# Seven products for seven more pairs of chunks in a first feed-forward, and 2x written into the banks of w_down

## The chip, the cores and the metric

The kernel runs on one core of a Trainium2 chip, without other cores at work. The metric is the device time of one execution in microseconds; the time before is the median of three runs.

TensorE multiplies a 128x128 stationary tile with 512 moving columns into a bank of its accumulation memory (PSUM, eight banks of 128x512 here). VectorE (DVE in the profile) and ScalarE (ACT) prepare operands and empty the banks. SyncE (SP) issues the loads of the weights.

## The reference, cut to what matters

```python
def swiglu(h, w_gate, w_up, w_down):
    return (jax.nn.silu(h @ w_gate) * (h @ w_up)) @ w_down

def reference(...):
    x = x + 0.5 * swiglu(rms_norm(x, ffn1_norm), ffn1_w_gate, ffn1_w_up, ffn1_w_down)
    x = gated_parallel_mixer(x, ...)
    x = memory_cross_attention(x, mem, ...)
    x = x + 0.5 * swiglu(rms_norm(x, ffn2_norm), ffn2_w_gate, ffn2_w_up, ffn2_w_down)
    return rms_norm(x, final_norm)
```

There are 256 tokens of width 2048, and the inner width of a feed-forward is 5632. Everything is float32. The change touches the first feed-forward, and the form of the `w_down` product in both.

## The kernel before

**Three matmuls for a product.** [...] A product of two split tiles is three matmuls (lines 442 to 444: `hi` by `hi`, `hi` by `lo`, `lo` by `hi`). The activations are split once. The weights are split as they come: ScalarE casts a raw tile to `hi` (L365), VectorE subtracts it from the raw tile to get `lo` (L366). `hi` and `lo` have three buffers each.

**Blocks and groups.** The inner width is cut into 11 blocks of 512 columns, numbered 0 to 10. They stand in three groups: blocks 0 to 3, 4 to 7, 8 to 10. A group first computes gate and up of its blocks, and then multiplies its part of the hidden activations with the matching rows of `w_down`, in two calls: output columns 0 to 1023, then 1024 to 2047. The result is added into `x`, which stays in SBUF.

**Pairs of chunks and seven products.** The inner dimension of a product is cut into chunks of 128, and two chunks are a pair. A pair in `product_pair` makes two token halves by two column blocks (gate and up, or two column blocks of `w_down`): eight products. A pair that is named in `seven` uses Winograd's form of Strassen's scheme instead, with seven products `p1` to `p7`. That needs four sums of the raw weight tiles on VectorE (L394 to L397, `raw<-raw`), the split of two tiles of sums (`thi` on ScalarE L373, `tlo` on VectorE L374, one buffer each), and combinations of the activations (`c` for the gate and up blocks, `d` for `w_down`), which a background task (`combinations`, lines 474 to 493) makes ahead. One product goes into each of the banks `p1` to `p7`; the pairs with eight products add into `p2`, `p4`, `p3` and `p5` for the four results. Since the banks of the seven products are shared between the results, a pair with eight products that comes before the last pair with seven must not add into `p5`. The blocks of gate and up get around this with combinations of the activations (`less` in line 555, pairs 1 and 3); `w_down` uses a further bank `q` (`to = "q"`).

Banks come in three rings: `mm` with three (`p1`, `p3`, `p5`), `acc` with three (`p2`, `p4`, `q`) and `tr` with two (`p6`, `p7`, and transposes).

```python
SEVEN, SEVEN_DOWN = (0, 2, 4), ((2, 4, 6), (2, 4))
```

So before, all of the blocks 1 to 10 in the first feed-forward take seven products for pairs 0, 2 and 4 of their eight; `w_down` does so for pairs 2, 4 and 6 in the first call of the two larger groups, and for pairs 2 and 4 otherwise. In the second feed-forward (`SEVEN_2`) it is pairs 0, 2, 3, 4.

**The ends of a block.** When the last pair with seven is done, `middle` combines `p1`, `p6`, `p7`, `p5` (L579 to L581, with `hb` copied by ScalarE in L576). After the last pair of the block, `out` adds each of `p2`, `p4`, `p3`, `p5` as it is finished (L588, Silu on ScalarE in L589, L592, L593): this is called the tail below. The result `hb` of a block is transposed on TensorE (L630) after the next block's `middle`, and split (`hhi` L635, `hlo` L636). For `w_down`, `first`, `middle` and `out` add into `x` (L603, L606, L611 to L613): 12 VectorE instructions and one of ScalarE in a call.

**What sets the order.** The program is written as one stream: `next_item` fetches the two weight tiles of a pair, loads what lies ahead, and splits the next pair as well (`AHEAD`), so that VectorE and ScalarE are one pair ahead of TensorE. A background task advances at each `bg.tick()`. From this stream, a scheduler of the framework makes the order on each engine, within the dependences; each engine then runs its own list strictly in that order. So an instruction that waits holds up what stands behind it on its engine.

## Time and profile before

| | us |
| --- | --- |
| median of three runs (2217.84 to 2219.36) | 2218.06 |
| the profiled execution | 2216.97 |
| its span, first to last instruction | 2215.2 |
| first feed-forward in it, about | 5 to 710 |
| blocks 0 to 3 and their `w_down` | 5 to 180, 180 to 265 |
| blocks 4 to 7 and their `w_down` | 265 to 433, 433 to 518 |
| blocks 8 to 10 and their `w_down` | 518 to 644, 644 to 710 |
| second feed-forward, its first `w_down` starts | 1679 |

The page gives busy times of each engine, then their shares in 40 slices of 55 us. A window gives the same for any stretch. The timeline lists instructions with start and length; on TensorE and VectorE the end of one overlaps the start of the next, so the price of an instruction is the distance between two starts and not its length. The row of a wait names the waiting instruction, what it waited for, the total, the count and the longest.

### The profile page before, as it was taken

The page shows a single profiled execution, that of the slowest core. Times are in us where ns is not written, and L with a number is a line of the kernel's source. Part 1 is how long each engine was busy: PE and PEld are TensorE (multiplying, and loading weights), DVE is VectorE, ACT ScalarE, POOL GpSimd, SP SyncE. Part 2 cuts the span into 40 slices and gives each one's busy share as a digit, 9 for nine tenths or more (in the row PEclk, how much of TensorE's full clock was granted, in tenths as well). Part 3 has the DMA queues.
Part 4 walks back from the last instruction along what each step waited for, and adds up shares of the span by engine and source line. Part 5 has one row for each costly group of instructions (what it writes and reads, how often), then busy time and mean ns, then how long its engine had stood idle before and what let it go on. Part 6 is the DMA issues. An engine that isn't in the chain of part 4 may idle for free.

```text
span 2215.2 us, 28140 instructions
## 1 busy us (share of the span) xinstructions
PE 2200.2 (99%) x10520; PEld 1817.0 (82%) x10520; DVE 1829.0 (83%) x2348; ACT 1250.0 (56%) x1621; POOL 107.0 (5%) x185
## 2 busy tenths in 40 slices
PE   9999999999999999999999999999999999999998
PEld 7888888888888877788888888888888888888886
DVE  7999988898989476977667666558999999999997
ACT  7555555555556477644544546556565565555654
POOL 0000000000000000000331130001000000000000
PEclk9999999999999999999999999999999999999999
DMA  8555555555556545676768687547665666665573
GB/s 306 199 207 198 194 200 201 198 199 194 200 194 204 178 130 165 197 237 210 223 224 287 209 273 270 183 164 280 220 221 190 212 227 211 214 208 208 200 244 135
DMA packets 231560, 466.02 MB, mean 210 GB/s; under 512 B 15520, under 2 KB 17920, under 8 KB 231424
## 3 DMA queue, kind: packets, MB, share of 16 engines
q1 hardware_dynamic: 222256, 438.08, 58.4%
q0 software_dynamic: 7648, 23.52, 3.5%
q10 hardware_dynamic: 1520, 2.63, 0.3%
q8 instruction: 82, 1.34, 0.3%
q14 instruction: 54, 0.44, 0.1%
HBM read 440.49 MB, written 23.59 MB: 209 GB/s over the span
## 4 chain that ended last, share of the span: by engine, by line
PE 94%; DVE 3%; DMA 1%; issue 1%; ACT 1%; SPq 0%; POOLq 0%; POOL 0%; DVEq 0%; ACTq 0%
PE acc L442 19%; PE acc L443 19%; PE acc L444 19%; PE mm L443 8%; PE mm L444 8%; PE mm L442 8%; PE tr L443 2%; PE tr L630 2%; PE tr L442 2%; PE tr L444 2%; PE mm L1425 1%; DVE lo L366 1%; DMA raw<-in_ffn_w_up_dram 1%; PE tr L1355 0%; ACT hi L365 0%
## 5 line engine op out<-in xcount | busy, mean ns | idle before, releaser
L365 ACT CAST hi<-raw 128x1024 fp32r<-128x1024 f32 (+1 forms) x768 | 755.1, 993 | 687.7 <-PE acc L444 485.9
L366 DVE TENSOR_TENSOR lo<-raw,hi 128x1024 fp32r<-128x1024 f32 (+1 forms) x768 | 878.8, 1147 | 291.8 <-ACT hi L365 289.3
L442 PE MATMUL acc<-hi,xhi 128*128 128x512 f32 (+1 forms) x1134 | 445.7, 394 | 2.0 <-DVE ga L1278 1.5
L443 PE MATMUL acc<-lo,xhi 128*128 128x512 f32 (+1 forms) x1134 | 439.9, 388 | 0.8 <-DVE lo L366 0.8
L444 PE MATMUL acc<-hi,xlo 128*128 128x512 f32 (+1 forms) x1134 | 439.7, 388 | 0.0
L442 PEld LDWEIGHTS acc<-hi,xhi 128*128 128x128 f32 x1134 | 213.2, 188 | 47.8 <-issue 3.1
L444 PEld LDWEIGHTS acc<-hi,xlo 128*128 128x128 f32 x1134 | 212.9, 188 | 43.5 <-issue 0.4
L443 PEld LDWEIGHTS acc<-lo,xhi 128*128 128x128 f32 x1134 | 213.4, 188 | 42.7 <-DVE lo L366 2.2
L373 ACT CAST thi<-raw 128x1024 fp32r<-128x1024 f32 x192 | 200.3, 1052 | 69.1 <-DVE raw L396 45.0
L374 DVE TENSOR_TENSOR tlo<-raw,thi 128x1024 fp32r<-128x1024 f32 x192 | 232.1, 1217 | 0.9 <-ACT thi L373 0.3
L442 PE MATMUL mm<-hi,xhi 128*128 128x512 f32 x402 | 156.6, 389 | 0.1
L443 PE MATMUL mm<-lo,xhi 128*128 128x512 f32 x402 | 156.5, 389 | 0.0
L444 PE MATMUL mm<-hi,xlo 128*128 128x512 f32 x402 | 156.4, 389 | 0.0
L444 PE MATMUL acc<-hi,hlo 128*128 128x512 f32 x372 | 145.4, 391 | 0.0
L443 PE MATMUL acc<-lo,hhi 128*128 128x512 f32 x372 | 145.3, 391 | 0.0
L442 PE MATMUL acc<-hi,hhi 128*128 128x512 f32 x372 | 145.0, 390 | 0.0
L442 PEld LDWEIGHTS mm<-hi,xhi 128*128 128x128 f32 x402 | 75.4, 188 | 16.2 <-ACT hi L365 0.5
L443 PEld LDWEIGHTS mm<-lo,xhi 128*128 128x128 f32 x402 | 75.5, 188 | 15.8
L444 PEld LDWEIGHTS mm<-hi,xlo 128*128 128x128 f32 x402 | 75.5, 188 | 15.7
L442 PEld LDWEIGHTS acc<-hi,hhi 128*128 128x128 f32 x372 | 69.9, 188 | 14.3
L443 PEld LDWEIGHTS acc<-lo,hhi 128*128 128x128 f32 x372 | 69.8, 188 | 14.3
L444 PEld LDWEIGHTS acc<-hi,hlo 128*128 128x128 f32 x372 | 69.9, 188 | 14.0
(443 smaller groups left out, 3526.6 us busy)
## 6 DMA issues: line engine op xcount, KB each, us to landing
raw<-in_ffn_w_down_dram SPq DMA_DIRECT2D x88, 1024.0 KB, 5.2
raw<-in_ffn_w_gate_dram SPq DMA_DIRECT2D x84, 1024.0 KB, 5.1
raw<-in_ffn_w_up_dram SPq DMA_DIRECT2D x78, 1024.0 KB, 6.0
raw<-in_w_in_dram SPq DMA_DIRECT2D x136, 512.0 KB, 3.8
raw<-in_w_out_dram SPq DMA_DIRECT2D x32, 512.0 KB, 4.7
raw<-sums SPq DMA_DIRECT2D x20, 512.0 KB, 6.2
raw<-in_w_proj_attn_dram SPq DMA_DIRECT2D x16, 512.0 KB, 4.0
raw<-in_w_proj_rwkv_dram SPq DMA_DIRECT2D x16, 512.0 KB, 5.7
```

Of the source, the lines that this page charges most:

```text
L365: at["hi"] = act.copy(hi[:, s], raw[:, s])
L366: at["lo"] = dve.tensor_tensor(lo[:, s], raw[:, s], f32(hi[:, s]), ALU.subtract)
L373: act.copy(hi[:], v[:])
L374: dve.tensor_tensor(lo[:], v[:], f32(hi[:]), ALU.subtract)
L442: pe.matmul(o, xh, hi, start=first, stop=False, **how)
L443: pe.matmul(o, xh, lo, start=False, stop=False, **how)
L444: pe.matmul(o, xl, hi, start=False, stop=last, **how)
L630: pe.transpose(b[:, o : o + P], tok[:, t, col : col + P], ident[:])
L1425: pe.matmul(vb[to, (o + k) * P : (o + k + 1) * P][:, r], lhs(k, e), v[:, k, r], start=v is u and k + e == 0, stop=True, **ek,)
```

## The change

It has four parts.

1. In the first feed-forward, the blocks 3, 5, 7, 9 and 10 take seven products for pairs 0, 2, 4, 6 (`SEVEN_MORE`), the blocks 4, 6 and 8 for pairs 2, 4, 6 (`SEVEN_LATER`); blocks 1 and 2 keep 0, 2, 4. The second call of `w_down` takes pairs 2, 4, 6 in the two larger groups. Counted: 5 blocks and 2 calls with one seven more, 7 in all. In blocks 4, 6 and 8 it is as many as before, at other pairs.
2. The combinations for pair 6 are made later than the others (from item 26 of the plan on, in block 2), and `combinations` gets the list of pairs with `less` explicitly. A block waits only for the combinations that it uses. A pair with eight products that has no `less` combination (pair 5, and pair 0 in the blocks that start later) adds its `p5` part into the bank `q`, so the eight blocks with pair 6 have one more VectorE instruction in their tail.
3. In `w_down`, in both feed-forwards, ScalarE first writes twice `x` into the banks `p2`, `p4`, `p3` and `q` (`onto`), and the matmuls add to it. `first` is one ScalarE instruction that writes half of `p1` over `x`, and `middle` and `out` are eight VectorE instructions instead of 12. Each call so has four ScalarE instructions more and four VectorE instructions fewer.
4. Two unused tiles (`shift`, `pad`) go, and `down` needs no tiles `u`.

```diff
 SEVEN, SEVEN_DOWN = (0, 2, 4), ((2, 4, 6), (2, 4))
+SEVEN_MORE, MORE = (0, 2, 4, 6), (3, 5, 7, 9, 10)
+SEVEN_LATER, LATER_ON = (2, 4, 6), (4, 6, 8)
...
-                yield (wg, wu), 0, KD, (j * 512, j * 512), SEVEN_2 if last else SEVEN
+                seven = SEVEN_MORE if j in MORE else SEVEN_LATER if j in LATER_ON else SEVEN
+                seven = SEVEN_2 if last else seven
+                yield (wg, wu), 0, KD, (j * 512, j * 512), seven
...
-            yield (wd, wd), 4 * j0, 4 * nj, (1024, 1536), SEVEN_DOWN[1]
+            yield (wd, wd), 4 * j0, 4 * nj, (1024, 1536), SEVEN_DOWN[last or nj < 4]
...
-    def product_pair(x: Act, c, w, first, middle, out):
+    def product_pair(x: Act, c, w, first, middle, out, onto=()):
...
+        for to, there in onto:
+            b[to] = rings[to]()
+            act.activation(b[to][:], there, AF.Copy, scale=2.0)
+            begun.add(to)
...
-                less = to == "p3" and early and c["early"]
-                if to == "p5" and early and not c["early"]:
+                less = to == "p3" and early and q in c["less"]
+                if to == "p5" and early and q not in c["less"]:
                     to = "q"
...
-                dve.tensor_tensor(v[:], b[to][:], v[:], ALU.add)
+                for z in (to, "q") if t and "q" in b else (to,):
+                    dve.tensor_tensor(v[:], b[z][:], v[:], ALU.add)
...
-    def down(sp, h: Act, c, w, xs):
-
-        u2, u3 = sums_of(sp)
-
-        def half(x_, v):
-            dve.scalar_tensor_tensor(x_, v, 0.5, x_, ALU.mult, ALU.add)
+    def down(h: Act, c, w, xs):
+
+        (x00, x01), (x10, x11) = xs
+
+        def half(x_, v, y):
+            dve.scalar_tensor_tensor(x_, v, 0.5, y, ALU.mult, ALU.add)
 
         def first(b):
-            act.copy(u3[:], b["p1"][:])
-            half(xs[0][0], b["p1"][:])
-            half(xs[1][1], b["q"][:])
+            act.activation(x00, b["p1"][:], AF.Copy, scale=0.5)
 
         def middle(b):
-            dve.tensor_tensor(u2[:], b["p6"][:], u3[:], ALU.add)
-            dve.tensor_tensor(u3[:], b["p7"][:], u2[:], ALU.add)
-            dve.tensor_tensor(u2[:], b["p5"][:], u2[:], ALU.add)
-            half(xs[1][0], u3[:])
-            half(xs[1][1], u3[:])
-            half(xs[0][1], u2[:])
+            half(x01, b["p6"][:], x00)
+            half(x10, b["p7"][:], x01)
+            half(x01, b["p5"][:], x01)
+            half(x11, b["q"][:], x10)
...
+        product_pair(
+            h, c, w, first, middle, out, (("p2", x00), ("p4", x10), ("p3", x01), ("q", x11))
+        )
...
-            sp, norm.x, SEVEN_2 if last else SEVEN, "c",
-            lambda: at["item"] > begun + (4 if last else 7) and not (last and norm.r is None),
+            sp, norm.x, SEVEN_2 if last else SEVEN_MORE, "c",
+            lambda q: (
+                at["item"] > begun + (4 if last else 26 if q > 4 else 7)
+                and not (last and norm.r is None)
+            ),
+            less=(1,) if last else (1, 3),
```

In the order that results, two places show what moves. The names end in the number of the tile; the lines of the changed program are a few higher (L366 becomes L368, L588 L594, L592 L599, L593 L600, L636 L642).

VectorE before, at the start of block 7: the last sums and splits of pair 0, the tail of block 6, then the gate's `lo` of pair 1.

```order
L374 TENSOR_TENSOR tlo_3212<-raw_3205,thi_3211 128x1024
L366 TENSOR_TENSOR lo_3216<-raw2_3113,hi_3215 128x1024
L374 TENSOR_TENSOR tlo_3224<-raw_3206,thi_3223 128x1024
L366 TENSOR_TENSOR lo_3220<-raw2_3169,hi_3219 128x512
L588 TENSOR_TENSOR hb_2910<-acc_2935,hb_2910 128x512
L588 TENSOR_TENSOR hb_2910<-acc_2943,u_2912 128x512
L592 TENSOR_TENSOR u_2911<-mm_2939,u_2911 128x512
L592 TENSOR_TENSOR u_2912<-mm_2947,u_2912 128x512
L593 SCALAR_TENSOR_TENSOR hb_2910<-u_2911,rs_450,hb_2910 128x512
L593 SCALAR_TENSOR_TENSOR hb_2910<-u_2912,rs_450,hb_2910 128x512
L366 TENSOR_TENSOR lo_3265<-raw2_3113,hi_3264 128x1024
```

VectorE after, at the same place. Ahead of these rows stand the splits of pair 0 and the first three of the tail and of the block's transposes (two L594, one L642). The last row is again the gate's `lo` of pair 1.

```order
L474 TENSOR_TENSOR raw_3267<-hhi_2250,hlo_2251 128x512
L642 TENSOR_TENSOR hlo_2251<-tr_3260,hhi_2250 128x512
L480 TENSOR_TENSOR raw_3267<-raw_3267 128x128
L482 TENSOR_TENSOR raw_3267<-raw_3267 128x128
L481 TENSOR_TENSOR raw_3267<-raw_3267 128x128
L599 TENSOR_TENSOR u_2938<-mm_2964,u_2938 128x512
L483 TENSOR_TENSOR raw_3267<-raw_3267 128x128
L600 SCALAR_TENSOR_TENSOR hb_2937<-u_2938,rs_448,hb_2937 128x512
L599 TENSOR_TENSOR u_2939<-mm_3020,u_2939 128x512
L493 TENSOR_TENSOR dlo_2253<-raw_3267,dhi_2252 128x512
L599 TENSOR_TENSOR u_2939<-acc_2971,u_2939 128x512
L368 TENSOR_TENSOR lo_3308<-raw2_3140,hi_3307 128x1024
```

Between the splits of pair 0 and the `lo` of pair 1 now also stand the second `hlo` of the transposed block, one whole combination (L474 to L493) and the add of the bank `q` (the last L599); one scaled add of the tail went behind the `lo`.

ScalarE before, at the end of block 3 and the start of `w_down`: casts of weights (`hi`), the two Silu of the tail (L589) and the casts of the transposed block (`hhi`).

```order
L365 CAST hi_1517<-raw2_1425 128x1024
L365 CAST hi_1521<-raw2_1481 128x1024
L589 ACTIVATE hb_1222<-hb_1222,rs_450 128x512 x2
L365 CAST hi_1561<-raw2_1425 128x1024
L635 CAST hhi_146<-tr_1576 128x512
L635 CAST hhi_146<-tr_1581 128x512
L365 CAST hi_1565<-raw2_1481 128x1024
```

ScalarE after, at the same place, with the writes from `x` into the banks `p2`, `p4` (acc_1576, acc_1578) and `q` (acc_1582).

```order
L367 CAST hi_1513<-raw2_1427 128x1024
L641 CAST hhi_144<-tr_1529 128x512
L641 CAST hhi_144<-tr_1534 128x512
L595 ACTIVATE hb_1228<-hb_1228,rs_448 128x512
L367 CAST hi_1517<-raw2_1476 128x1024
L595 ACTIVATE hb_1228<-hb_1228,rs_448 128x512
L515 ACTIVATE acc_1576<-x_106 128x512
L515 ACTIVATE acc_1578<-x_106 128x512
L367 CAST hi_1586<-raw2_1427 128x1024
L490 CAST dhi_146<-raw_1541 128x512
L367 CAST hi_1590<-raw2_1476 128x1024
L515 ACTIVATE acc_1582<-x_106 128x512
```

The writes into `p2` and `p4` stand behind both Silu and ahead of the casts of the second pair of `w_down`; the write into `q` stands behind them and ahead of the casts of the third.

28 lines of the change are left out of this document (13 added, 15 removed).

## The prediction

> **What bounds the kernel now.** I read the page first: busy shares, then the slices, then the waits of TensorE, then the first feed-forward by windows, then single instructions in the timeline.
>
> ```profile
> span 2215.2 us, 28140 instructions
> PE 2200.2 (99%) x10520; PEld 1817.0 (82%) x10520; DVE 1829.0 (83%) x2348; ACT 1250.0 (56%) x1621; POOL 107.0 (5%) x185
> PE   9999999999999999999999999999999999999998
> DVE  7999988898989476977667666558999999999997
> ```
>
> TensorE has work all the time, so an instruction taken from it is worth its full slot. But VectorE has hardly less to do in the first thirteen slices, where the change is made. A window over the first feed-forward and the waits of TensorE say how much room is left:
>
> ```profile
> 50.00:710.00 660.00, 659.68 (x2957) 544.70 (x2956) 605.48 (x752) 369.32 (x421) 1.47 (x2) 1.00 0.57 197
> PE tr L1007 <- DVE s L998: 1.6, 1, 1.6
> PE acc L443 <- DVE lo L366: 0.8, 2, 0.5
> ```
>
> The columns are length, then busy time of TensorE, its weight loads, VectorE, ScalarE, GpSimd, then the granted clock. VectorE is busy 605.5 of 660 us, 92%; TensorE waits for it almost never. It can't run far ahead, though: it writes its `lo` tiles into three buffers and its `tlo` tiles into single ones, so it is one item ahead at most. What counts is the head start: by how much a `lo` tile is ready before the first matmul that reads it.
>
> Prices come from the distances between starts, since the ends overlap. First TensorE, then eight transposes among matmuls, then VectorE at the start of block 7:
>
> ```profile
> 221.64 0.39 PE L444 MATMUL mm<-hi,hlo 128*128 128x512 f32 x1
> ...
> 225.27 0.39 PE L442 MATMUL mm<-hi,hhi 128*128 128x512 f32 x1
> 121.55 1.03 PE L630 MATMUL tr<-ident,hb 128*128 128x128 f32 x8
> 122.66 0.40 PE L443 MATMUL acc<-lo,xhi 128*128 128x512 f32 x1
> 384.72 1.22 DVE L366 TENSOR_TENSOR lo<-raw,hi 128x1024 fp32r<-128x1024 f32 x1
> 385.85 0.68 DVE L397 TENSOR_TENSOR raw<-raw,raw 128x512 f32<-128x512 f32 x1
> 386.46 1.22 DVE L374 TENSOR_TENSOR tlo<-raw,thi 128x1024 fp32r<-128x1024 f32 x1
> 387.59 1.22 DVE L366 TENSOR_TENSOR lo<-raw,hi 128x1024 fp32r<-128x1024 f32 x1
> 388.73 1.22 DVE L374 TENSOR_TENSOR tlo<-raw,thi 128x1024 fp32r<-128x1024 f32 x1
> 389.86 0.68 DVE L366 TENSOR_TENSOR lo<-raw,hi 128x512 fp32r<-128x512 f32 x1
> 390.46 0.68 DVE L588 TENSOR_TENSOR hb<-acc,hb 128x512 f32<-128x512 f32 x1
> 391.06 0.68 DVE L588 TENSOR_TENSOR hb<-acc,u 128x512 f32<-128x512 f32 x1
> 391.66 1.28 DVE L592 TENSOR_TENSOR u<-mm,u 128x512 f32<-128x512 f32 x2
> 392.89 1.41 DVE L593 SCALAR_TENSOR_TENSOR hb<-u,rs,hb 128x512 f32<-128x512 f32 x2
> 394.22 1.22 DVE L366 TENSOR_TENSOR lo<-raw,hi 128x1024 fp32r<-128x1024 f32 x1
> 652.10 0.28 DVE L482 TENSOR_TENSOR raw<-raw 128x128 f32<-128x128 f32 x1
> 652.30 0.29 DVE L481 TENSOR_TENSOR raw<-raw 128x128 f32<-128x128 f32 x1
> ```
>
> - TensorE: 16 matmuls from 221.64 to 225.27, 0.227 us each. A product is three of them, 0.68 us. Eight transposes: 122.66 - 121.55 - 0.23 = 0.88 us.
> - VectorE: 0.60 us for 512 columns (389.86 to 390.46), 1.136 for 1024, 0.66 for a scaled add (392.89 to 394.22 for two), 0.20 for 128.
>
> So an item with eight products ("plain") takes TensorE 24 x 0.227 = 5.44 us and VectorE two `lo`, 2.27 us. An item with seven takes TensorE 4.76 us and VectorE four sums, two `tlo`, a `lo` and half a one: 5 x 0.60 + 3 x 1.136 = 6.42 us. Each new seven thus saves TensorE 0.68 us and costs VectorE 4.15 us.
>
> **The change part by part.**
>
> *Seven pairs.* 7 x 3 = 21 matmuls fewer: -21 x 0.227 = -4.8 us. In the same feed-forward VectorE gets 7 x 4.15 = 29.0 us, one more add in eight blocks (the bank `q`, 8 x 0.60 = 4.8) and the combinations of pair 6 (0.60 + 4 x 0.20 + 0.60 = 2.0); the six calls of `w_down` lose four instructions each (-14.4). Net +21.4 us on 605.5, with TensorE's time 4.8 shorter: about 96%. It fits on average, so the places decide.
>
> *Start of block 7.* The head start at the `lo` that limits there follows by a walk. In the rows above VectorE is ready at 384.72 + 1.22 = 385.94 with the last `lo` of block 6 and at 395.44 with the gate's `lo` of pair 1. TensorE's first uses of the two:
>
> ```profile
> 388.44 0.39 PE L443 MATMUL mm<-lo,xhi 128*128 128x512 f32 x1
> 395.92 0.39 PE L443 MATMUL acc<-lo,xhi 128*128 128x512 f32 x1
> ```
>
> The head start falls from 2.50 to 0.48 us. By prices: 2.50 + 7.48 of TensorE - 9.48 of VectorE = 0.50, so the walk holds. After the change the last seven of block 6 is pair 6, its tail comes late, and VectorE has 22 instructions between the same two tiles: 13 of 512 columns, four of 1024, four of 128 and one scaled add, 7.83 + 4.54 + 0.81 + 0.66 = 13.8 us (seven of them the head of the block, two `hlo`, six of a combination, six of the tail of block 6, the `lo` itself). TensorE has 37 matmuls, 8.4 us. A last `lo` behind a seven and eight transposes has at most this head start, as in block 3:
>
> ```profile
> 162.08 1.21 DVE L366 TENSOR_TENSOR lo<-raw,hi 128x1024 fp32r<-128x1024 f32 x1
> 166.49 0.39 PE L443 MATMUL mm<-lo,xhi 128*128 128x512 f32 x1
> ```
>
> 166.49 - 163.29 = 3.2 us. So 3.2 + 8.4 - 13.8: TensorE waits 2.2 us. Bounds 1.0 and 3.5 (a head start of 4.4, or of 1.9).
>
> *Start of block 10.* The same without the combination and with one sum before the stretch: 12.4 against 8.4 us, 3.2 + 8.4 - 12.4: it waits 0.8 us (0 to 2.1). Blocks 5 and 9 have a plain start of the block ahead of them, and the same walk ends at +0.2 us there.
>
> *Three entries into `w_down`* (behind blocks 3, 7, 10). Today one is already tight:
>
> ```profile
> 191.66 1.22 DVE L374 TENSOR_TENSOR tlo<-raw,thi 128x1024 fp32r<-128x1024 f32 x1
> 192.57 0.39 PE L444 MATMUL mm<-hi,hlo 128*128 128x512 f32 x1
> 192.93 0.50 PE L443 MATMUL tr<-tlo,dhi 128*128 128x512 f32 x1
> 193.27 0.39 PE L444 MATMUL tr<-thi,dlo 128*128 128x512 f32 x1
> ```
>
> The steps 0.36 and 0.34 instead of 0.227 lose 0.25 us. Now two combinations instead of one, the tail and two `hlo` fall between the second `lo` of the call and its first `tlo`: 14 of 512, four of 1024, two scaled adds and eight of 128 columns, 15.9 us, against 12.0 of TensorE (49 matmuls and eight transposes). 3.2 + 12.0 - 15.9 = -0.7; less the 0.25 that is lost already, 3 x 0.47 = +1.4 us (0 to 4).
>
> *ScalarE's writes.* No row shows a write from SBUF into a bank; the nearest are these:
>
> ```profile
> L589 ACT ACTIVATE hb<-hb,rs 128x512 f32<-128x512 f32 x40 | 27.4, 718 | 7.2 <-DVE hb L588 7.2
> L490 ACT CAST dhi<-raw 128x512 fp32r<-128x512 f32 x16 | 10.0, 622 | 16.2 <-DVE raw L483 16.2
> L606 ACT COPY u<-mm 128x512 f32<-128x512 f32 x11 | 6.5, 587 | 10.4 <-PE mm L444 10.4
> ```
>
> I take 0.62 us, the source being SBUF (0.59 to 0.72). 44 of them, 27 us on an engine that is busy 56%, cost nothing as such. But `p2` is the first bank that TensorE fills in a call, and its write waits for VectorE's last read of the bank, behind two Silu and a cast of 1024 columns in ScalarE's queue; casts stand behind it. By walk the write ends 0.3 us before its use and that of `q` as it is needed: 0.2 us each, 3 x 0.2 = +0.6. If the whole chain of 0.72 + 1.05 + 0.72 + 0.62 = 3.1 us were open it would be 9.3; below, 0. The other eight calls (the second halves, and the second feed-forward, whose blocks leave a bank of three free) have over 1.5 us: nothing.
>
> *Tight running.* Pairs 0, 2, 4, 6 leave VectorE 10.2 - 8.7 = 1.5 us in every two items, so after each of these places it stays near 0 for some items. About six more `tlo` come with under 0.25 us; at the 0.25 us lost above that is +1.5 (0 to 5).
>
> *The rest.* The four VectorE instructions that each call in the second feed-forward loses stand behind its tight entry: 0 (at best -1). The removed tiles hold no instruction: 0.
>
> Sum: -4.8 + 2.2 + 0.8 + 1.4 + 0.6 + 1.5 = +1.7 us on the profiled execution of 2216.97 us (span 2215.2 and 1.8 around it). That execution is 1.1 below the median 2218.06, so the median becomes 2219.8; I say 2220.
>
> [...]
>
> **The rivals.**
>
> 1. *Faster: VectorE hides it all.* TensorE loses nothing, 2218.06 - 4.8 = 2213.3. For it: 92% busy, and waits of 0.8 us in the whole run. Against it: the walk at block 7, which needs a head start of 5.4 us where rows show 3.2. Chance 0.09.
> 2. *Slower: the write into `p2` comes late.* From 1 us to the whole 3.1 at the three entries and 0.5 at the other three calls of the first feed-forward: +4.5 to +10.8 in place of 0.6, so 2224 to 2230. It decides once VectorE's last read of the bank slips by over 0.3 us behind the crowded stretch. Chance 0.13.
> 3. *Slower: near 0 throughout.* In blocks 3, 5, 7, 9, 10 each of 20 sevens loses 0.25 us, 5.0 instead of 1.5: 2223.5. For it: ScalarE and VectorE hand tiles to and fro, and the walk has no gap between instructions. Chance 0.11.
> 4. *Slower: an instruction occupies VectorE for its whole duration where it waits for ScalarE's cast each time.* The starts are then 0.68 apart, 22 x 0.08 = 1.8 us more at each of five places: 2229. The spacing at 385 to 394 us speaks against it. [...] Chance 0.06.
> 5. [...] Chance 0.04.
>
> **How the numbers follow.** The forecast has 0.57, with its own range 2216 to 2223. A change under 0.2% (4.4 us, 2213.6 to 2222.5) can't be told from none here. Faster: rival 1, 0.09. Within: the forecast but for 0.02, and half of rival 5, 0.57. Slower: 0.02 + 0.02 + 0.13 + 0.11 + 0.06 = 0.34. The range 2215 to 2226.5 leaves out rival 1, rival 4 and the upper part of rival 2, some 0.2.
>
> **What would show it.** Right: 21 matmuls fewer; VectorE near 96% from 50 to 705 us; waits of TensorE for `lo` and `tlo` of some 6 us in all, the longest, about 2 us, at the start of block 7, some 390 us into the span, others at the three entries. The writes into banks show as 44 ScalarE rows of about 0.6 us. Wrong: TensorE waiting for ScalarE's writes, waits in the second feed-forward, or a longest wait at another place; no waits at all would mean that the head start is larger than the rows say.

## The result and the profile after

The changed kernel takes 2230.62 us (median of four runs, 2229.42 to 2231.1) against 2218.26 us. The ratio is 1.0054, with a 95% interval of 1.0042 to 1.0067: slower by 12.4 us, outside the forecast range (2215 to 2226.5). The profiled execution has a span of 2229.1 us, 13.9 more than before.

The same lines of the page as for the kernel before:

```profile
span 2229.1 us, 28202 instructions
PE 2203.0 (99%) x10499; PEld 1810.8 (81%) x10499; DVE 1836.1 (82%) x2360; ACT 1281.6 (57%) x1680; POOL 107.3 (5%) x185
PE   9999999999999999999999999999999999999998
DVE  7999899998999476978657666558999899998996
```

TensorE has the 21 matmuls fewer (10520 to 10499), and VectorE 7.1 us more work. The busy share of TensorE still reads 99%: in the rows below a matmul is 0.39 us long and the next starts 0.227 us after it, so a wait of a tenth of a us leaves no gap in the record, and the shares don't show the loss. The window over the first feed-forward, and the waits of TensorE:

```profile
50.00:705.00 655.00, 646.22 (x2868) 526.72 (x2867) 611.19 (x771) 384.10 (x451) 1.89 (x3) 1.00 0.59 197
```

```profile
PE acc L444 <- ACT hi L367: 3.0, 4, 0.9
PE acc L445 <- DVE lo L368: 1.7, 3, 0.9
...
PE acc L444 <- DVE hb L594: 1.5, 3, 0.6
...
PE mm L444 <- ACT hi L367: 1.3, 3, 0.4
PE tr L636 <- DVE u L586: 1.2, 1, 1.2
...
PE mm L445 <- DVE lo L368: 1.1, 3, 0.4
```

VectorE is busy 611.2 of 655 us, 93%, where 96% was forecast. Its work came out as forecast (627.0 us from 50 to 722 us, for 605.5 + 21.4); the time did not get shorter. And the waits are not for VectorE's `lo` and `tlo` alone: the longest in total is for ScalarE's casts (`hi`), and reads of banks in the tail (L594) and in `middle` (L586) stand among them.

To place the loss I compare the time from the first matmul with a combination of `x` (in block 1) to the last with `hhi` (in the last call of `w_down`). In the kernel before:

```profile
52.08 0.73 PE L442 MATMUL tr<-thi,chi 128*128 128x512 f32 x2 [0.26 <-ACT thi L373]
...
709.65 0.39 PE L443 MATMUL mm<-lo,hhi 128*128 128x512 f32 x1
```

In the changed kernel:

```profile
53.07 0.73 PE L444 MATMUL tr<-thi,chi 128*128 128x512 f32 x2 [0.26 <-ACT thi L375]
...
720.96 0.39 PE L445 MATMUL mm<-lo,hhi 128*128 128x512 f32 x1
```

That is 657.6 us before and 667.9 after, 10.3 more although 21 matmuls (4.8 us) are gone. So 15.1 us of waits were added in this stretch. The other 3.6 us of the span lie in front of it (1.0) and behind it (2.6), where the profiles of the other kernels differ from the one before by up to 2.2 and by -0.6 to 2.8 us too. Behind it two waits are new in this execution, 1.1 us for `x` (L1612) and 0.9 us for a `tlo` in the second feed-forward; e7's profile has both and e16's neither, so I leave them out and explain only the 15.1. The table of the experiments gives this figure for every kernel ("added waits": difference of that stretch to 657.6, plus 0.227 us for each matmul saved).

TensorE's rows give the places; a wait is the distance of two starts less 0.227 us. At the entry into `w_down` behind block 3:

```profile
193.96 0.39 PE L444 MATMUL mm<-hi,dhi 128*128 128x512 f32 x1
194.18 0.39 PE L444 MATMUL acc<-hi,hhi 128*128 128x512 f32 x1
195.25 0.50 PE L444 MATMUL acc<-hi,hhi 128*128 128x512 f32 x1 [0.68 <-ACT hi L367]
196.12 0.50 PE L445 MATMUL mm<-lo,dhi 128*128 128x512 f32 x1 [0.36 <-DVE lo L368]
196.46 0.40 PE L446 MATMUL mm<-hi,dlo 128*128 128x512 f32 x1
196.69 0.39 PE L444 MATMUL mm<-hi,hhi 128*128 128x512 f32 x1
196.93 0.63 PE L444 MATMUL tr<-thi,dhi 128*128 128x512 f32 x2
197.99 0.49 PE L444 MATMUL mm<-hi,hhi 128*128 128x512 f32 x1 [0.44 <-ACT hi L367]
198.46 0.50 PE L445 MATMUL tr<-tlo,dhi 128*128 128x512 f32 x1
198.79 0.39 PE L446 MATMUL tr<-thi,dlo 128*128 128x512 f32 x1
```

Nine steps (the row at 196.93 holds two matmuls) take 4.61 us from 194.18 to 198.79 instead of 2.04: 2.55 us. The entries behind blocks 7 and 10 lose as much to within 0.05 us. Before, 0.21 to 0.25 us were lost at each, so 3 x 2.3 = 6.9 us are new. The other places, in the same profile:

| place | added, us | what TensorE waits for |
| --- | --- | --- |
| three entries into `w_down` | 6.9 | casts `hi`, then `lo` |
| end of block 6 and start of block 7 | 4.2 | 1.4 at the transposes, 0.5 at a bank of `acc`, 1.1 and smaller for `lo` and sums |
| start of block 10 | 1.0 | a bank of `acc`, freed by the tail |
| start of block 5 | 1.1 | the same |
| all the rest | 1.9 | waits under 0.3 us each |

### The profile page after: what moved, and what is told of

Its sections match the earlier page's. It is cut to its first block, busy times and chain, and to the rows that moved or that the text cites. A ratio compares the mean times of both kernels' runs of the same rounds, so it can differ in the third digit from the quotient of the medians.

```text
span 2229.1 us, 28202 instructions
## 1 busy us (share of the span) xinstructions
PE 2203.0 (99%) x10499; PEld 1810.8 (81%) x10499; DVE 1836.1 (82%) x2360; ACT 1281.6 (57%) x1680; POOL 107.3 (5%) x185
## 4 chain that ended last, share of the span: by engine, by line
PE 87%; DVE 7%; DMA 3%; ACT 1%; issue 1%; SPq 0%; POOLq 0%; POOL 0%; DVEq 0%; ACTq 0%
PE acc L444 18%; PE acc L445 18%; PE acc L446 18%; PE mm L445 7%; PE mm L446 7%; PE mm L444 7%; DVE lo L368 2%; DMA raw<-in_ffn_w_up_dram 2%; PE tr L445 2%; PE tr L446 2%; PE tr L636 2%; PE tr L444 2%; PE mm L1435 1%; ACT hi L367 1%; DVE tlo L376 1%
## 5 line engine op out<-in xcount | busy, mean ns | idle before, releaser
L368 DVE TENSOR_TENSOR lo<-raw,hi 128x1024 fp32r<-128x1024 f32 (+1 forms) x768 | 874.6, 1144 | 280.4 <-ACT hi L367 278.0
L375 ACT CAST thi<-raw 128x1024 fp32r<-128x1024 f32 x206 | 214.8, 1051 | 78.0 <-DVE raw L398 50.8
L376 DVE TENSOR_TENSOR tlo<-raw,thi 128x1024 fp32r<-128x1024 f32 x206 | 249.7, 1219 | 1.2 <-ACT thi L375 0.6
L445 PE MATMUL mm<-lo,xhi 128*128 128x512 f32 x365 | 142.2, 390 | 0.0
L446 PE MATMUL mm<-hi,xlo 128*128 128x512 f32 x365 | 142.1, 389 | 0.0
L444 PE MATMUL mm<-hi,xhi 128*128 128x512 f32 x365 | 141.6, 390 | 0.0
L396 DVE TENSOR_TENSOR raw<-raw,raw 128x512 f32<-128x512 f32 x93 | 63.9, 687 | 33.8 <-DMA raw<-in_ffn_w_up_dram 23.5
L444 PEld LDWEIGHTS mm<-hi,xhi 128*128 128x128 f32 x365 | 68.5, 188 | 14.9 <-ACT hi L367 0.5
L445 PEld LDWEIGHTS mm<-lo,xhi 128*128 128x128 f32 x365 | 68.5, 188 | 14.3
```

The source lines that it names most:

```text
L368: at["lo"] = dve.tensor_tensor(lo[:, s], raw[:, s], f32(hi[:, s]), ALU.subtract)
L375: act.copy(hi[:], v[:])
L376: dve.tensor_tensor(lo[:], v[:], f32(hi[:]), ALU.subtract)
L396: dve.tensor_tensor(t[1][:, 0], ru[:, 0], rg[:, 0], ALU.subtract)
L444: pe.matmul(o, xh, hi, start=first, stop=False, **how)
L445: pe.matmul(o, xh, lo, start=False, stop=False, **how)
```

## The experiments

| kernel | us (median) | ratio to before, 95% | matmuls | added waits, us |
| --- | --- | --- | --- | --- |
| before | 2217.64 to 2218.48 beside them | 1 | 0 | 0 |
| changed | 2230.62 | 1.0042 to 1.0067 | -21 | 15.1 |
| e1 no writes | 2229.64 | 1.0037 to 1.0063 | -21 | 16.9 |
| e2 writes alone | 2218.09 | 0.9991 to 1.0008 | 0 | 0.6 |
| e3 no write into q | 2229.39 | 1.0034 to 1.0062 | -21 | 15.3 |
| e4 no gate pairs | 2218.81 | 0.9992 to 1.0010 | -6 | 2.7 |
| e5 second calls alone | 2222.80 | 1.0012 to 1.0030 | -6 | 5.9 |
| e7 blocks 4, 6, 8 as before | 2227.37 | 1.0029 to 1.0057 | -21 | 12.8 |
| e8 no second calls | 2228.74 | 1.0038 to 1.0064 | -15 | 15.2 |
| e11 q read early | 2226.54 | 1.0028 to 1.0053 | -21 | 11.5 |
| e12 and banks turned | 2226.65 | 1.0027 to 1.0053 | -21 | 11.9 |
| e13 no subtractions | 2230.46 | 1.0042 to 1.0067 | -21 | 15.7 |
| e14 load alone | 2218.46 | 0.9992 to 1.0010 | 0 | 0.2 |
| e16 q early, block 6 as before | 2223.47 | 1.0016 to 1.0034 | -21 | 9.2 |
| e17 second calls, 4 and 8 later | 2220.42 | 1.0000 to 1.0017 | -6 | 2.2 |
| e18 pair 6 without q | 2231.05 | 1.0042 to 1.0070 | -6 | 12.8 |
| e19 pair 6 with q | 2226.47 | 1.0027 to 1.0052 | -6 | 10.3 |
| e20 four sevens without q | 2220.43 | 1.0003 to 1.0020 | -9 (-3 in the whole program) | 3.7 |
| e23 blocks 5 and 9, q early | 2222.78 | 1.0011 to 1.0029 | -12 | 7.6 |
| e24 fourth pair at 5 | 2219.71 | 0.9998 to 1.0016 | -15 | 3.1 |

An interval is some 4 to 6 us wide, so two kernels that lie 2 us apart are not told apart by their times. The added waits come from one execution each.

### Which part of the change costs

*e4: the gate blocks as before.*

```diff
-SEVEN_MORE, MORE = (0, 2, 4, 6), (3, 5, 7, 9, 10)
-SEVEN_LATER, LATER_ON = (2, 4, 6), (4, 6, 8)
+SEVEN_MORE, MORE = (0, 2, 4, 6), ()
+SEVEN_LATER, LATER_ON = (2, 4, 6), ()
...
-            sp, norm.x, SEVEN_2 if last else SEVEN_MORE, "c",
+            sp, norm.x, SEVEN_2 if last else SEVEN, "c",
```

> Part 1 and the moved pairs undone: the gate blocks take seven products at pairs 0, 2 and 4 as before, which takes five of the seven added pairs away; the two added pairs in w_down's second calls and ScalarE's writes stay. Theories A and B agree that the loss starts in the gate blocks: the two pairs that are left save 6 matmuls of 0.227 us, 1.4 us, so 2217 us, and the losses at the entries, at the transposes of block 7 and at the starts of blocks 5, 7 and 10 are all gone. If the loss were w_down's own (its second calls or the writes), it would stay at 2226 to 2230 us.

2218.81 us: the loss is gone with the pairs in the gate blocks. The 1.4 us of six matmuls did not come out: two waits for w_down's last addition (0.83 and 0.94 us) stand at the starts of blocks 4 and 8.

*e1, e2, e3: the writes of 2x.* e1 is the changed kernel with the old `down`; e2 is the kernel before with the new `down` and `onto`, no new pair; e3 leaves only the write into `q` out:

```diff
         def first(b):
             act.activation(x00, b["p1"][:], AF.Copy, scale=0.5)
+            half(x11, b["q"][:], x11)
...
-            half(x11, b["q"][:], x10)
+            dve.tensor_tensor(x11, x11, x10, ALU.add)
...
-            h, c, w, first, middle, out, (("p2", x00), ("p4", x10), ("p3", x01), ("q", x11))
+            h, c, w, first, middle, out, (("p2", x00), ("p4", x10), ("p3", x01))
```

> Part 3 undone: the changed kernel with w_down's old `first`, `middle` and `out`, so that ScalarE writes no 2x into the banks and VectorE adds x with instructions of its own, while all seven added pairs stay. The profile of the changed kernel shows some 2.3 us of TensorE waits at each entry into w_down. Theory A (a hand-off chain: a product queued behind ScalarE's write of 2x keeps an `hi` buffer, ScalarE's next casts wait for that buffer, and VectorE and TensorE wait for the casts): the write into `q` goes, and with it most of the three entries' loss, about 2 us each; 2230.6 - 6 = 2224 to 2225 us. Theory B (VectorE simply has too much to do, and the writes relieve it): without the writes VectorE has about 1.2 us more per call, so the time gets no better, 2230 to 2236 us.

> Part 3 alone: the kernel before, with ScalarE's writes of 2x into p2, p4, p3 and q at each call of w_down, and none of the added pairs. Theory A: in the kernel before the gate blocks use no bank for q, so the write into q waits for a bank that came free long ago, and the queues have slack: 2217 to 2219 us, no change. Theory B: the same, or a little better, since VectorE has less to do. Rival 2 of the prediction (the writes themselves come late at each entry, with or without the added pairs) gives 2221 to 2228 us.

> The changed kernel, in which ScalarE writes 2x into p2, p4 and p3 as before, but not into q; VectorE adds x11 with one more instruction in `first` and one more in `middle`. Theory A (the write into q, behind the gate block's last read of q's bank, is the link): the entries' loss goes as without any writes, about 2224.5 us. Theory B: the write into q is one of 44 cheap instructions, VectorE gets about 0.6 us more per call: 2230 to 2232 us. If the writes into p2, p4 and p3 are what counts, nothing changes either, 2230.6 us, while the kernel with no writes at all gets faster.

2229.64, 2218.09 and 2229.39 us. On balance the writes do no harm, neither by themselves nor beside the new pairs, and theory A in its first form (the write is the link) falls. At the entries the steps still add to 2.0 us each in e1 and in e3, against 2.55; the 0.5 us that the write into `q` may cost there are lost at other places, since the added waits of the whole stretch are no smaller (16.9 and 15.3). ScalarE's rows show why the entries stay dear. First the changed kernel, then e1, both at the entry behind block 3:

```profile
186.25 0.60 ACT L515 ACTIVATE acc<-x 128x512 f32<-128x512 f32 x1 [1.24 <-DVE u L599]
188.74 1.05 ACT L367 CAST hi<-raw 128x1024 fp32r<-128x1024 f32 x1 [1.89 <-PE acc L446]
```

```profile
184.24 1.05 ACT L367 CAST hi<-raw 128x1024 fp32r<-128x1024 f32 x1
188.35 1.05 ACT L367 CAST hi<-raw 128x1024 fp32r<-128x1024 f32 x1 [3.06 <-PE acc L446]
```

With or without the write, the cast that comes next ends its wait with a matmul into `acc`. By the names of the tiles that cast writes into a `hi` buffer whose last reader is w_down's first product into `q`. The scheduler has put that product on TensorE behind the second pair's products into `p2` and `p4`, late enough for the bank `q` of block 3 to be read by the tail's last addition (starting at 185.53); its last matmul starts at 188.26, and the cast at 188.74. What VectorE does meanwhile, in the changed kernel:

```profile
185.53 0.68 DVE L599 TENSOR_TENSOR u<-acc,u 128x512 f32<-128x512 f32 x1
186.13 1.22 DVE L368 TENSOR_TENSOR lo<-raw,hi 128x1024 fp32r<-128x1024 f32 x1
187.26 0.75 DVE L600 SCALAR_TENSOR_TENSOR hb<-u,rs,hb 128x512 f32<-128x512 f32 x1
189.82 1.22 DVE L368 TENSOR_TENSOR lo<-raw,hi 128x1024 fp32r<-128x1024 f32 x1 [1.81 <-ACT hi L367]
```

It stands idle for 1.81 us, in the middle of what the prediction took for its most crowded stretch, and TensorE's loss follows some 7 us later.

*e5 and e8: the second calls of w_down.* e5 adds only these pairs to the kernel before; e8 takes them out of the changed one.

```diff
-            yield (wd, wd), 4 * j0, 4 * nj, (1024, 1536), SEVEN_DOWN[1]
+            yield (wd, wd), 4 * j0, 4 * nj, (1024, 1536), SEVEN_DOWN[last or nj < 4]
```

> The kernel before with only the two added pairs in w_down's second calls of groups 0 and 1 (sevens at pairs 2, 4 and 6), no writes of 2x, no other pair. They save 6 matmuls, 1.36 us. Together with the writes they gave 2218.81 us, not below 2218.37 us, and the profile of that kernel has two TensorE waits of 0.83 and 0.94 us at the starts of blocks 4 and 8 for VectorE's last addition of w_down (the p2 bank read in the tail). Theory A: the same waits here, since pair 6 puts four reads of banks just ahead of the tail: 2218 to 2219 us. If the writes of 2x cause these waits, the saving stays: 2217 us.

> Part 2 undone: the changed kernel without the two added pairs in w_down's second calls of groups 0 and 1; the five pairs in the gate blocks, the moved pairs and the writes of 2x stay. Six matmuls more, 1.36 us. In the profile of the changed kernel no TensorE wait of 0.15 us or more stands in the second calls or at the starts of blocks 4 and 8, so these two pairs are bought for nothing there: 2231.5 to 2232.5 us. If they cost there what they cost alone (2222.8 against 2218 us): 2226 to 2228 us.

e5 takes 2222.80 us, 4.8 more than before: alone, these two pairs cost. With the writes of 2x (e4) they cost nothing that can be measured; the intervals of e5 and e4 don't touch. So the writes, which leave VectorE eight instructions in a call instead of 12, are worth some 4 us there. At the starts of blocks 4 and 8 TensorE's list has 1.8 us for w_down's `x` and 1.3 us for `tlo` in e5, and 1.4 us for `x` alone in e4. Whether the two pairs cost anything in the changed kernel stays open: e8's profile has 1.5 us more in the first feed-forward, as their matmuls would make it, but its median is 1.9 us lower.

### VectorE's load

*e13* leaves the four subtractions of an added pair out; *e14* adds idle work to the kernel before; `light` and `heavy` hold pair 6 of blocks 3, 5, 7, 9 and 10.

```diff
         t = summed.get(i)
+        if i in light:
+            t = raws[g], raws[u]
```

```diff
         if not seven:
+            if i in heavy:
+                for _ in range(7):
+                    dve.tensor_tensor(spare[:], raws[u][:, 1], raws[g][:, 0], ALU.subtract)
             parts[i] = split_unit(g), split_unit(u)
```

> The changed kernel with its seven pairs and its banks, but the four subtractions that form the weights of an added pair are left out at pair 6 of blocks 3, 5, 7, 9 and 10 (the raw tiles are multiplied in their place, so those blocks compute something else, with as many products, casts and transfers). That takes 20 subtractions of 0.60 us, 12 us, off VectorE in FFN1, 2.4 us in each of the five blocks. In the profile of the changed kernel these blocks hold 41.3 to 43.1 us of VectorE work against some 41.4 us of TensorE work. Theory B (a block with four pairs of sevens has more VectorE work than TensorE work, and the buffers carry little of it into the next block): 2.4 us less brings them to 39 to 40.7 us, and nearly all is gained: 2217 to 2221 us. Theory A (banks handed on in fixed places, q's above all): the entries and the block starts stay as they are but for VectorE's lag at them: 2226 to 2230 us.

> The kernel before, with nothing of the change, and seven idle subtractions of 128x512 into a spare tile at pair 6 of blocks 3, 5, 7, 9 and 10: 7 x 0.60 = 4.2 us of VectorE work in each, about what an added pair brings (6.7 us of VectorE for a pair of sevens by its rows, 2.4 us for a plain one). No matmul goes, no bank q is used in these blocks. Theory B: the same loss as in the changed kernel without its saved matmuls, 2.5 to 3 us for each of the five, 2228 to 2233 us. Theory A: VectorE has 35.2 to 38.5 us of work in these blocks before, so with 4.2 us more it still just fits in 42.1 us: 2218 to 2221 us.

2230.46 and 2218.46 us. Theory B, the load of a whole block, falls twice. Block 7 in the changed kernel and in e13, columns as in the window above:

```profile
396.00:440.20 44.20, 42.61 (x188) 33.89 (x187) 43.09 (x58) 27.06 (x33) 0.00 (x0) 1.00 0.57 191
```

```profile
396.00:440.20 44.20, 42.59 (x188) 33.85 (x188) 40.70 (x54) 26.21 (x31) 0.00 (x0) 1.00 0.56 190
```

2.4 us of VectorE's work are gone in this block, and its length is the same. At the entry behind block 3, e13's waits are those of the changed kernel (its lines are a few higher):

```profile
ACT hi L370 <- PE acc L451: 3.7, 3, 1.9
DVE lo L371 <- ACT hi L370: 1.8, 1, 1.8
...
PE acc L449 <- ACT hi L370: 0.7, 1, 0.7
```

And in e14 VectorE is busy 41.5 of 43 us around block 5, 97%, and TensorE all the time:

```profile
308.00:351.00 43.00, 43.00 (x196) 35.70 (x195) 41.52 (x53) 23.74 (x27) 0.00 (x0) 1.00 0.59 196
```

### The bank q

*e11* reads `q` in `middle` instead of at the end of the tail, with the same number of instructions; *e12* also hands out the three banks of `acc` in another turn.

```diff
             dve.tensor_tensor(u2[:], b["p5"][:], u2[:], ALU.add)
+            if "q" in b:
+                dve.tensor_tensor(hb[:, 1], b["q"][:], u3[:], ALU.add)
...
-                for z in (to, "q") if t and "q" in b else (to,):
-                    dve.tensor_tensor(v[:], b[z][:], v[:], ALU.add)
+                dve.tensor_tensor(v[:], b[to][:], v[:], ALU.add)
```

```diff
-        return ps.tile([P, 512], F32, tag="acc", name="acc")
+        i = at["acc"] = at.get("acc", -1) + 1
+        return ps.tile([P, 512], F32, tag=f"acc{i % 3}", name="acc", bufs=1)
...
+        if "q" in b:
+            at["acc"] += 2
```

> All seven added pairs and the writes of 2x stay; in gate blocks that use a bank q, VectorE reads q in `middle`, right behind the last seven products, and no longer behind p5 at the end of the tail. The number of VectorE instructions is the same, only the place of one of them moves. Theory A is recast, since neither taking away ScalarE's writes (2229.64 us) nor that into q alone (2229.39 us) brought the time down: it is the bank itself. A gate block with q uses all three `acc` banks, and its q is read last of all, so w_down's q product, in whatever way x is added, cannot start before that read; the product stands late in TensorE's order and keeps its `hi` buffer from ScalarE's casts. By that the three entries lose almost nothing with q read early: three times 1.5 to 2.3 us less, 2224 to 2226 us. Theory B (VectorE has more work in the gate blocks than the blocks last, wherever it stands): 2229 to 2231 us.

> As the run before (q read in `middle`), and the three `acc` banks are given out in another turn: after a call that used q, the next p2 gets the bank of that q, which was read early, and not that of the same block's p2, which is read in the tail just ahead of it. Theory A (banks): beside the entries, the TensorE waits at the starts of blocks 5, 7 and 10 for VectorE's tail go (0.70 + 0.50 + 0.77 us and some 0.1 us behind each in the profile of the changed kernel): 2 us less than the run before, 2222 to 2224 us; what is left is the start of block 7 with 1.4 us at the transposes and some 2 us behind it. Theory B (VectorE's load): 2229 to 2231 us.

2226.54 and 2226.65 us. Moving one addition in eight blocks brings 4.1 us back; turning the banks brings nothing more. TensorE's waits at the entry behind block 3 in e11, and the rows where its steps are longer than 0.227 us:

```profile
PE tr L444 <- ACT thi L375: 0.2, 1, 0.2
192.84 0.39 PE L444 MATMUL mm<-hi,dhi 128*128 128x512 f32 x1
...
194.70 0.73 PE L444 MATMUL tr<-thi,dhi 128*128 128x512 f32 x2 [0.17 <-ACT thi L375]
...
196.53 0.39 PE L445 MATMUL tr<-tlo,dhi 128*128 128x512 f32 x1
```

The waits listed there fall from 1.5 us (0.68, 0.36 and 0.44 in the rows of the changed kernel) to 0.2. By the steps the fall is smaller: eleven of them take 3.69 us from 192.84 to 196.53 instead of 2.49, so 1.2 us are lost, against 2.55 in the changed kernel and 0.25 before; behind blocks 7 and 10 it is 1.1. So the late read of `q` makes some 1.4 of the 2.3 us that each entry lost, 4.2 in all, which is about what the time fell by. The other 0.9 us stay at each entry. There VectorE runs from 179.10 to 194.48 us without a listed wait, and e18 below, which has no `q`, loses the same 1.1 us at each entry. The second half of theory A fell: in e12 the starts of blocks 5 and 7 keep waits of 0.9 and 0.7 us, now at `p4` and at a bank of `tr`.

### Where the last pair with seven stands

*e7* and *e16* put back blocks 4, 6 and 8, or block 6 alone on top of e11:

```diff
-SEVEN_LATER, LATER_ON = (2, 4, 6), (4, 6, 8)
+SEVEN_LATER, LATER_ON = (2, 4, 6), ()
```

```diff
-SEVEN_LATER, LATER_ON = (2, 4, 6), (4, 6, 8)
+SEVEN_LATER, LATER_ON = (2, 4, 6), (4, 8)
```

> The changed kernel, in which blocks 4, 6 and 8 take their seven products at pairs 0, 2 and 4 as before, and not at 2, 4 and 6: the same number of matmuls and of VectorE's instructions as in the changed kernel. Theory A (places where a bank is handed on): block 6 no longer reads p6 and p7 just ahead of its transposes, so the 1.39 us at the transposes before block 7 go, and the waits behind them get shorter; the entries stay: 2227 to 2228.5 us. Theory B (load alone): the place does not matter, 2229.5 to 2231.5 us. The prediction's own step 2 (VectorE gets three runs of sevens in a row without rest, in which blocks 4, 6 and 8 play no part but the last pair): 2230 us too.

> q read in `middle` (2226.54 us), and beside it block 6 alone takes 0, 2 and 4 as before; blocks 4 and 8 keep 2, 4 and 6, since with 0, 2 and 4 they waited 0.94 us each at their starts for w_down's tail. If the two gains are of different places (the entries by q, the start of block 7 by block 6), they add: 2226.5 - 3 = 2222.5 to 2224.5 us. If both only give VectorE the same bit of room, they do not: 2226 us. By theory B neither brings it under the 2218 us of the kernel before, since the four-seven blocks stay.

2227.37 and 2223.47 us, as theory A said. With block 6 as before, the 4.2 us around block 7 are gone; in e7, where blocks 4 and 8 are put back too, two waits of 0.94 us came at the starts of these (15.1 - 4.2 + 1.9 = 12.8). In the changed kernel they begin with these rows:

```profile
389.17 0.60 PE L636 MATMUL tr<-ident,hb 128*128 128x128 f32 x4
390.99 0.66 PE L636 MATMUL tr<-ident,hb 128*128 128x128 f32 x4 [1.23 <-DVE u L586]
```

Block 6 has its last sevens at pair 6, so `middle` reads `p6` and `p7` just when the transposes of block 5 need the same two banks of `tr`. In e16 the gains of e11 and of block 6 add, and the loss is down to 5.2 us.

*e17* has the second calls' pairs, the writes, and blocks 4 and 8 at 2, 4 and 6 (`LATER_ON = (4, 8)`, `MORE = ()`).

> No block with four pairs of sevens: the two added pairs of w_down's second calls, the writes of 2x, and blocks 4 and 8 at 2, 4 and 6. The run without any gate pairs gave 2218.81 us with two TensorE waits of 0.83 and 0.94 us at the starts of blocks 4 and 8, where the first pair is one of sevens. If moving those pairs is what the first pair needs, 1.8 us go and the 1.4 us of six matmuls are kept: 2216.5 to 2217.5 us, a little faster than the kernel before. If pair 6 of these blocks is no better a place: 2218 to 2220 us.

2220.42 us. The waits at blocks 4 and 8 went, one of 0.57 us came at the start of block 5; the times of e17 and e4 can't be told apart. It is no gain.

*e18* and *e19* take no fourth pair. In e18 all blocks from 1 on have 0, 2 and 6 and no `q`; in e19 the five blocks have 0, 2 and 6, with `q`. Beside the lines shown, a block in e18, e19 and e20 waits only for the sums of `x` of pairs ahead of its last seven, and e18 makes all combinations early.

```diff
-SEVEN, SEVEN_DOWN = (0, 2, 4), ((2, 4, 6), (2, 4))
-SEVEN_MORE, MORE = (0, 2, 4, 6), (3, 5, 7, 9, 10)
-SEVEN_LATER, LATER_ON = (2, 4, 6), (4, 6, 8)
+SEVEN, SEVEN_DOWN = (0, 2, 6), ((2, 4, 6), (2, 4))
+SEVEN_MORE, MORE = (0, 2, 6), ()
+SEVEN_LATER, LATER_ON = (0, 2, 6), ()
...
-            less=(1,) if last else (1, 3),
+            less=(1,) if last else (1, 3, 4, 5),
```

```diff
-SEVEN_MORE, MORE = (0, 2, 4, 6), (3, 5, 7, 9, 10)
-SEVEN_LATER, LATER_ON = (2, 4, 6), (4, 6, 8)
+SEVEN_MORE, MORE = (0, 2, 4, 6), ()
+SEVEN_LATER, LATER_ON = (0, 2, 6), (3, 5, 7, 9, 10)
```

> As many products as the kernel before, and its w_down (with the writes of 2x, which alone changed nothing), but all gate blocks from 1 on take seven products at pairs 0, 2 and 6 in place of 0, 2 and 4, and their plain pairs 1, 3, 4 and 5 all use sums of x, so that no bank q is needed. VectorE's load as a cause has fallen (35 idle subtractions cost nothing, 20 subtractions fewer gained nothing). Theory D (the bank: with q a gate block uses all three `acc` banks, and each hand-over at its end is late): no q, no loss, 2217 to 2219 us. Theory E (the place: with the last sevens at pair 6, VectorE's reads of p6, p7 and p5, those of the tail, and the first sevens of the next block fall into the same few us, whatever banks there are): a loss at each of ten block ends of 1 to 2 us, 2228 to 2238 us.

> As many products as the kernel before and its w_down with the writes of 2x; blocks 3, 5, 7, 9 and 10 take seven products at 0, 2 and 6 in place of 0, 2 and 4, and their pairs 4 and 5 use the bank q, read behind p5 at the end of the tail as in the changed kernel. No block has four pairs of sevens. Theories D and E both expect the changed kernel's waits here (bank q and the place both stand): its loss without its saving, five times 2.5 to 3 us: 2229 to 2233 us. If it is 2220 us or less, four pairs in one block are needed for the loss, and the load is back in the play in some local form.

The two texts are wrong in one point: in both kernels the pairs of w_down's second calls stood, so they have six matmuls fewer than the kernel before, and their control is e4 (2218.81 us, 2.7 us of added waits). Against it e18 loses 12.2 us and e19 7.7 us. Both bank and place cost:

- In e19 (three pairs of sevens, `q` read late) the entry behind block 3 has again the waits of the changed kernel, and the three entries hold nearly all of the 7.6 us of waits beyond e4:

```profile
ACT hi L367 <- PE acc L446: 3.7, 3, 1.9
DVE lo L368 <- ACT hi L367: 1.8, 1, 1.8
...
PE acc L444 <- ACT hi L367: 0.7, 1, 0.7
```

- In e18 (no `q`) the waits beyond e4 are 10.1 us; about 1.5 of them stand at the start of block 1, where more combinations have to be ready. The rest, some 0.9 us on average for each of ten block ends, is spread unevenly. It includes 0.9 us at each entry into `w_down` and the wait for the banks of `tr` that block 6 showed, here again without any `q`:

```profile
394.86 0.60 PE L636 MATMUL tr<-ident,hb 128*128 128x128 f32 x4
...
396.56 0.66 PE L636 MATMUL tr<-ident,hb 128*128 128x128 f32 x4 [0.64 <-DVE u L586]
```

*e20, e23, e24: can the pairs be had cheaper?* e20 has the five pairs without `q` (pair 5 takes sums of `x`), with pairs 2 and 4 in all calls of `w_down` to make room; e23 is e11 with added pairs in blocks 5 and 9 alone; e24 has the five pairs at pair 5 instead of 6, without `q`.

```diff
-SEVEN, SEVEN_DOWN = (0, 2, 4), ((2, 4, 6), (2, 4))
+SEVEN, SEVEN_DOWN = (0, 2, 4), ((2, 4), (2, 4))
-SEVEN_LATER, LATER_ON = (2, 4, 6), (4, 6, 8)
+SEVEN_LATER, LATER_ON = (2, 4, 6), ()
...
-            less=(1,) if last else (1, 3),
+            less=(1,) if last else (1, 3, 5),
```

```diff
-SEVEN_MORE, MORE = (0, 2, 4, 6), (3, 5, 7, 9, 10)
-SEVEN_LATER, LATER_ON = (2, 4, 6), (4, 6, 8)
+SEVEN_MORE, MORE = (0, 2, 4, 6), (5, 9)
+SEVEN_LATER, LATER_ON = (2, 4, 6), ()
```

```diff
-SEVEN_MORE, MORE = (0, 2, 4, 6), (3, 5, 7, 9, 10)
-SEVEN_LATER, LATER_ON = (2, 4, 6), (4, 6, 8)
+SEVEN_MORE, MORE = (0, 2, 4, 5), (3, 5, 7, 9, 10)
+SEVEN_LATER, LATER_ON = (2, 4, 6), ()
...
-            yield (wd, wd), 4 * j0, 4 * nj, (1024, 1536), SEVEN_DOWN[last or nj < 4]
+            yield (wd, wd), 4 * j0, 4 * nj, (1024, 1536), SEVEN_DOWN[1]
```

> The five added pairs in the gate blocks without bank q: pair 5 uses sums of x as pairs 1 and 3 do. To make room for these sums, all calls of w_down take seven products at pairs 2 and 4 only, and blocks 4, 6 and 8 are as before. Matmuls: 15 fewer by the five pairs, 6 more by pair 6 of w_down's first calls in groups 0 and 1, so 9 x 0.227 = 2.0 us fewer than the kernel before. Theory D (bank q): 2216 to 2217.5 us, faster than before. Theory E (the place, pair 6 ahead of the tail): the waits at the ends of five blocks stay, though p2's bank is free: 2222 to 2227 us.

> What is left when every place that the runs showed to be dear is avoided: added pairs in the gate blocks 5 and 9 alone (neither is followed by w_down), q read in `middle`, blocks 4, 6 and 8 as before, no added pairs in w_down, the writes of 2x as in the changed kernel. Two pairs save 6 matmuls, 1.36 us. By the runs so far a block end with pair 6 and q read early costs about 1 us where no w_down follows: 2 us in all, so 2218 to 2219.5 us, no faster than the kernel before. If the cost comes from the entries and from block 7 alone: 2216.5 to 2217.5 us, and this is the version that beats both.

> The five added gate pairs at another place: blocks 3, 5, 7, 9 and 10 take seven products at pairs 0, 2, 4 and 5 in place of 0, 2, 4 and 6, so that two plain pairs stand between the last sevens and the block's end, and pairs 1 and 3 use sums of x, so that no bank q is needed. Blocks 4, 6 and 8 and w_down's second calls are as in the kernel before, the writes of 2x stay. 15 matmuls fewer than the kernel before, 3.4 us. Theory E (the place directly ahead of the tail) together with theory D (bank q): both are gone, so 2215 to 2216.5 us, faster than both kernels. If two pairs of sevens in a row starve TensorE (12 to 13 us of VectorE's work in 9.5 us of TensorE's, and the buffers hold about a pair and a half), the waits only move: 2217 to 2221 us. By VectorE's load over the whole block, which has fallen, it would be 2226 us or more.

2220.43, 2222.78 and 2219.71 us. In e23 too the pairs of the second calls stood, against its text; against e4 its two pairs lose 4.0 us, so even with `q` read early a pair at 6 in the middle of a group is dear. e20 and e24, without `q`, are the cheapest ways of adding five pairs: 3.7 and 3.1 us of waits, while the matmuls save 2.0 and 3.4 us there. e20's text overlooks that the first calls of `w_down` in the second feed-forward lose pair 6 too: six matmuls, 1.4 us more, so that the whole program has 10517 matmuls, three fewer than before. Up to 1.4 of its 2.8 us over the kernel before can come from these. In e24's profile one single wait is listed between 60 and 711 us, and the span is 12.4 us shorter than that of the changed kernel:

```profile
PE tr L444 <- DVE xlo L693: 0.6, 1, 0.6
```

```profile
span 2216.7 us, 28181 instructions
```

But e24 is no faster than the kernel before (0.9998 to 1.0016). No version tried beats it. Some 0.6 to 0.7 us for each added pair remain even without `q`, in waits too small to be listed; their cause was not settled. e20 and e24 differ in more than the place, so they don't give a price of pair 6 against pair 5.

## Why the prediction was wrong

It said 2220 us, and the kernel takes 2230.6. By its terms:

| term | forecast, us | measured, us |
| --- | --- | --- |
| 21 matmuls | -4.8 | -4.8 |
| start of block 7 | +2.2 | +4.2 |
| start of block 10 | +0.8 | +1.0 |
| three entries into `w_down` | +1.4 | +6.9 |
| ScalarE's writes | +0.6 | 0 on balance (e1, e2, e3) |
| tight running (measured: all the rest) | +1.5 | +1.9 |
| start of block 5 | 0 | +1.1 |

The measured terms add to 10.3, the growth of the first feed-forward in the profile; the other 2 us of the 12.4 lie outside it and are not explained.

- **The step that failed is the entries.** The places were right, the term was mis-sized: 6.9 for 1.4, above its bound of 4. The walk added up VectorE's instructions between two tiles and let VectorE run without a gap. These rows bound the same stretch in the changed kernel, the second `lo` of the call with its first use, and the first `tlo` (first used at 198.46, above):

```profile
179.39 1.22 DVE L368 TENSOR_TENSOR lo<-raw,hi 128x1024 fp32r<-128x1024 f32 x1
183.93 0.39 PE L445 MATMUL mm<-lo,hhi 128*128 128x512 f32 x1
197.18 1.22 DVE L376 TENSOR_TENSOR tlo<-raw,thi 128x1024 fp32r<-128x1024 f32 x1
```

  The `lo` is ready at 179.39 + 1.22 = 180.61 and the `tlo` at 197.18 + 1.22 = 198.40. So the head start is 183.93 - 180.61 = 3.3 us, where the walk took 3.2, and VectorE needs 198.40 - 180.61 = 17.8 us, where it had 15.9. All but 0.1 of the difference is the 1.81 us in which VectorE stands idle in that very stretch. With them the walk's own sum is 3.2 + 12.0 - 17.7 = -2.5, and 2.55 us were lost. VectorE waits because a buffer of `hi` stays taken: its last reader is the product into `q`, and that product stands behind others on TensorE since the bank `q` was given a late last reader. The prediction counted the addition of `q` as 0.60 us of VectorE's time, and not as the moment that frees a bank. e11 moves this addition and takes 4.1 us off; e19 brings the entries' waits about with no product more. What stays in e11 at the three entries, 0.9 us each, lies within the term's bounds (0 to 4). So the crowding that the walk counted is probably a part of the loss; no run takes instructions out of this stretch itself, since the subtractions that e13 leaves out and e14 adds stand elsewhere.
- **Start of block 7.** The last `lo` of the walk is waited for, as forecast, and the 1.1 us there and the smaller waits ahead of it come near 2.2. What was not seen is the wait of 1.4 us at the transposes of block 5 and one of 0.5 us at a bank of `acc`. The banks of `tr` and `acc` were not followed at all, though the prediction named the rings.
- **Starts of blocks 5 and 10.** Block 10's size came out by luck; its reason is another: `p2` of the next block needs a bank that the tail has yet to read, since a block with `q` uses all three. By the same cause block 5 waits, where the walk had found +0.2 us to spare. Block 9 stands in the same way and loses only 0.3 us; why was not settled.
- **Tight running.** The size of what is left came near, but not as forecast: six `tlo` late by some 0.25 us were expected, and outside the entries the steps show one that is new, 0.24 us at 118.31. The rest is spread over steps of a tenth of a us and less.
- **ScalarE's writes.** Their duration was right: the forecast took 0.62 us, these rows show 0.58 and 0.60 (lowest, median and highest duration in ns):

```profile
L515 ACT ACTIVATE acc<-x x33: 575/584/604, 179.8 to 2155.4; 128x512 f32<-128x512 f32 x33
L515 ACT ACTIVATE mm<-x x11: 595/602/604, 172.4 to 2137.0; 128x512 f32<-128x512 f32 x11
```

  The write into `p2` does not hold the entry; rival 2, whose range (2224 to 2230) ends nearest to the time, had the wrong mechanism, as e1 shows: without any write the entries still lose 2.0 us each. Nor did the prediction see that these writes help: with the second calls' pairs they are worth 4 us (e5 against e4).
- **The other rivals.** Rival 4 ended at 2229, but its mechanism is refuted by the rows quoted above: the starts at 185.53 and 186.13 are 0.60 us apart, and the first of the two lasts 0.68. Rival 5, a lower clock after a wait, had a chance of 0.04, and the sum of the chances uses half of it; no run shows such a drop, nor a figure for it. In the changed kernel no wait in the first feed-forward exceeds 1.4 us and the longest in the whole profile is 1.6; the granted clock is 1.00 from 50 to 705 us and 0.999 on average over the span.

## What to carry to other kernels

Ask of an added read of a bank or a buffer not how long it takes but what it sets free, and what stands behind the next user of that in each engine's order: here one addition at the end of a block, 0.60 us long, held a bank, a product, a cast and then VectorE and TensorE, some 1.4 us at each of three places. VectorE, busy 92% of the first feed-forward before, took 23.9 us more work there without a loss of time (e14, 97% around block 5), and 2.4 us less in a block gained nothing (e13); so test a load theory by adding idle work to the kernel before. Work that ends in a shared bank goes where plain items follow it, and not directly ahead of the tail and the transposes.
